# Two unused 32-byte tiles around the split x in SBUF

## The chip, the cores and the metric

The kernel runs on one core of a Trainium2 chip. The metric is the device time of one execution in microseconds (us), the median of several runs. Five engines work side by side, each through its own queue in order: TensorE (PE; its weight loads are shown apart as PEld), VectorE (DVE), ScalarE (ACT), GpSimd (POOL) and SyncE (SP), which here issues all the transfers. Data lies in SBUF, 128 partitions wide; "offset" below means the byte at which a tile begins in every partition. Products are accumulated in PSUM.

## The reference

One layer of a decoder trunk on x of 256 tokens by 1024 features, all in float32: an RMSNorm with gain, one projection to q, k, v and z, causal attention of 16 heads of 64 with ALiBi, a gate by silu(z), an output projection, the residual, and a final RMSNorm. With 256 tokens there is only one block of the block-sparse attention, so it is plain causal softmax attention.

```python
hn = rms_norm(x, norm_g)
q, k, v, z = split(hn @ w_in, 4)                 # 1024 x 4096
logits = (q . k) * 64**-0.5 - slope[h] * (t - s), masked where s > t
o = softmax(logits) @ v                          # 16 heads
h = x + (o * silu(z)) @ w_out                    # 1024 x 1024
out = rms_norm(h, final_g)
```

## The kernel before

Every dense product runs as three float32r products: an operand `a` is split into a high part `ah` and a low part `al`, and `a @ b` is taken as `ah@bh + ah@bl + al@bh`. x is transposed, multiplied by the gain and split once into `xh` and `xl` (tiles of 128 x 8 x 256, lines 121 and 122, written by `x_split`). The weights come in pieces of 1 MB through five buffers `rawt`; ACT casts a piece to its high part `wh` (line 439) and DVE subtracts that to give the low part `wl` (line 441), two units ahead of their use, into four buffers each.

The program is a list of dense units, which PE works through in order:

- v0: the first half of v, as its weights land (lines 348 to 350). Its stationary operand is xh or xl, its moving operand 512 columns of wh or wl.
- eight z units, "c" units (`cols_unit`, lines 198 to 200). Stationary: 128 columns of wh or wl. Moving: 256 columns of xh or xl. 24 products a unit.
- four v units (lines 224 to 226 by `rows_mm`), operands as in v0.
- sixteen c units, q and k of eight pairs of heads in turn. Beside them runs the attention.
- o1 and o2, the output projection (lines 224 to 226 again). Stationary: 128 columns of gh or gl, the split gated attention. Moving: wh or wl, 512 columns at a time, but for one 512-wide block of the second token tile, which is taken in two pieces of 256 columns (`PIECES`).

The work beside the dense products is put into the engines' queues at places given by the table `SCH`, in steps of a quarter unit. A pair's chain there is: q and k out of PSUM by DVE (`qf` line 237, `kf` line 251), split by ACT (lines 241, 255, 256) and DVE (lines 245, 260); scores on PE (`sc`, lines 281 and 283); softmax on DVE (line 291), ACT (298) and DVE (304, 306); transposes on PE (`pt`, 312) and copy by ACT (`pT`, 316); product with v on PE (`ot`, 324); gate on DVE (331), its split on ACT (334) and POOL (335). The two weight splits of a pair stand among these on ACT and DVE, in a fixed order. With `sc=12.47` the scores of pair 0 are issued after the first of four steps, so after six products, of the fourth q/k unit.

Tiles are placed in a pool one after the other, each rounded up to 32 bytes. The offsets in the two built programs:

| tile | before | modulo 64 | modulo 128 | after | modulo 64 | modulo 128 |
|---|---|---|---|---|---|---|
| xh, xl | 44224, 52416 | 0 | 64 | 44256, 52448 | 32 | 96 |
| gh, gl | 78048, 86240 | 32 | 96 | 78112, 86304 | 32 | 32 |
| wh, wl (first of four) | 139680, 156064 | 32 | 32 | 139744, 156128 | 32 | 96 |

All slices that the dense products take of these tiles begin at whole multiples of 512 bytes in them.

Of the kernel before, what the change touches and what calls it, by code (L numbers as in the profile page):

```python
# [8 lines left out]
F32 = mybir.dt.float32  # L9
# [9 lines left out]
P = 128  # L19
# [3 lines left out]
MASKED = 3.0e38  # L23
# Where the work beside the dense products is issued, in dense steps (four per unit) from the first step of a
# pair's q unit. ha, la, hb, lb: high and low parts of the weights of two units to come; hq .. lk: of q and k; sc: scores; per head sm: maximum and exponential, no: normalisation, pt: transpose,
# ph: its copy; pv: product with v; ga, gs: gate and its split.
SCH = dict(ha=1.26, la=3.94, hb=8.91, lb=9.56, hq=4.5, lq=5.61, hk=9.09, lk=10.02, sc=12.47, sm0=12.72, sm1=13.22,
           no0=14.14, no1=14.86, pt0=17.85, ph0=17.92, pt1=19.42, ph1=19.89, pv=20.6, ga=21.77, gs=23.88)
# column pieces of the output's 512-wide blocks, by token tile and block: the last one ends in a short piece
WHOLE = [slice(0, 512)]  # L30
# [4 lines left out]
def hybrid_trunk(ctx: ExitStack, tc: tile.TileContext, x, norm_g, w_in, w_out, final_g, out):  # L35
    """One MoBA layer over a single block (so causal ALiBi softmax attention), gated by silu(z).

    Dense products run as float32r passes: an operand a is split exactly into ah + al, each of
    12 significant bits, and a @ b = ah @ bh + al @ bh + ah @ bl, accumulated in float32.
    The pre-norm's 1/rms is a factor per token and is applied to the projections' outputs.  # L40
    Attention runs in plain float32.
    """
    nc = tc.nc
# [5 lines left out]
    one = ctx.enter_context(tc.tile_pool(name="one", bufs=1))  # L49
# [3 lines left out]
    sm = ctx.enter_context(tc.tile_pool(name="sm", bufs=4))  # L53
    ps = ctx.enter_context(tc.tile_pool(name="ps", bufs=1, space=bass.MemoryType.PSUM))
    ctx.enter_context(tc.manual_schedule())

# [1 line left out]
    xs = [one.tile([P, D], F32, name=f"xs{j}") for j in range(NS)]  # L58
# [7 lines left out]
    def load_cols(c, half):  # L66
        """Columns c*512 + half*256 .. +256 of w_in, all rows."""
        t = raw.tile([P, ND, 256], F32, name="rawt")
        raws[c, half] = t
        lo = c * 512 + half * 256  # L70
        nc.sync.dma_start(t, wi[:, :, lo:lo + 256])

    def load_rows(key, w, c, t0, n=4, step=2):
        """Row tiles t0 .. t0+n of columns c*512 .. +512."""
        t = raw.tile([P, 4, 512], F32, name="rawt")
        raws[key] = t
        for i in range(0, n, step):
            nc.sync.dma_start(t[:, i:i + step, :], w[:, t0 + i:t0 + i + step, c * 512:(c + 1) * 512])

# [1 line left out]
    warm = one.tile([P, 512], BF16, name="warm")  # L81
# [6 lines left out]
    nc.vector.memset(mhalf, -0.5)  # L88
    # dist[p, c] = 128 + p - c where c <= 128 + p, else huge
    dist = one.tile([P, S], F32, name="dist")  # L90
# [27 lines left out]

# [1 line left out]
    gps = ps.tile([P, ND], F32, name="gps", tag="pt", bufs=1)  # L120
    xh = one.tile([P, ND, S], F32R, name="xh")
    xl = one.tile([P, ND, S], F32R, name="xl")
    gT = one.tile([P, ND], F32, name="gT")
    rbc = one.tile([P, S], F32, name="rbc")
    zs = one.tile([P, ND, S], F32, name="zs")
    v = one.tile([P, NS, D], F32, name="v")
# [3 lines left out]

# [1 line left out]
    wps = ps.tile([P, 512], F32, name="wps", tag="ot", bufs=1)  # L132
# [6 lines left out]

# [1 line left out]
    xt = {}  # L141

    def x_transpose(j, b, i0=0, i1=4):
        """Row tiles 4b+i0 .. 4b+i1-1 of x's token tile j; neighbours in different PSUM banks."""
        for n in range(2):
            if i0 == 0:
                xt[j, b, n] = ps.tile([P, 2, P], F32, name="xt", tag="acc", bufs=4)
        for i in range(i0, i1):
            d = 4 * b + i
            nc.tensor.transpose(xt[j, b, i % 2][:, i // 2, :], xs[j][:, d * P:(d + 1) * P], ident)  # L150
# [23 lines left out]

# [1 line left out]
    wh, wl = {}, {}  # L176
# [12 lines left out]
    def split_rows(key, i, parts=1):  # L189
        """Row tiles 2i, 2i+1 of a half chunk."""  # L190
        return split((key, i), raws[key][:, 2 * i:2 * i + 2, :], [P, 2, 512], parts)

    held = {}       # accumulators that are read later
    late = []       # issued after the next unit's weight split

# [1 line left out]
    def mm3(acc, ah, al, bh, bl, start, stop):  # L197
# [20 lines left out]
    def rows_mm(acc, key, i, ah, al, t0, j, start, stop, cols=slice(0, 512)):  # L218
        """acc += (row tiles t0, t0+1 of the stationary operand) x (split piece)."""
        w_h, w_l = wh[key, i], wl[key, i]  # L220
        for n in range(2):
            lh = ah[:, t0 + n, j * P:(j + 1) * P]
            ll = al[:, t0 + n, j * P:(j + 1) * P]
            nc.tensor.matmul(acc, lh, w_h[:, n, cols], start=start and n == 0, stop=False)  # L224
            nc.tensor.matmul(acc, lh, w_l[:, n, cols], start=False, stop=False)  # L225
            nc.tensor.matmul(acc, ll, w_h[:, n, cols], start=False, stop=stop and n == 1)  # L226
            yield

    # q and k of a pair of heads (A in partitions 0-63, B in 64-127), split in two and laid out so that
    # one product over 128 partitions gives qh kh + ql kh and one over 64 gives qh kl  # L230
    qf, kf, qq, kk, kl = {}, {}, {}, {}, {}
# [38 lines left out]

# [1 line left out]
    sc, nl, mn, pe_, sums, rs, pn, pt, pT, ot = {}, {}, {}, {}, {}, {}, {}, {}, {}, {}  # L272

    def scores(p):
        """Heads A and B in turn, so that their products over 64 partitions can share the array."""
        for a in range(2):
            sc[2 * p + a] = ps.tile([P, 384], F32, name="sc", tag="sc", bufs=2)
        for o, q, k in ((slice(0, 128), slice(0, 128), slice(0, 128)),
                        (slice(128, 384), slice(128, 256), slice(0, 256))):
            for a in range(2):  # L280
                nc.tensor.matmul(sc[2 * p + a][:, o], qq[p][:, a, q], kk[p][:, a, k], start=True, stop=False)  # L281
            for a in range(2):
                nc.tensor.matmul(sc[2 * p + a][:, o], qq[p][HALF[a], a, q], kl[p][HALF[a], k], start=False, stop=True)  # L283
# [34 lines left out]
    def pv(p):  # L318
        """The two heads side by side, each in its half of the columns."""
        ot[p] = ps.tile([P, S], F32, name="ot", tag="ot", bufs=1)  # L320
        for j, o, q in ((0, slice(0, S), slice(0, S)), (1, slice(P, S), slice(S, 384))):
            for a in range(2):
                h = 2 * p + a
                nc.tensor.matmul(ot[p][HALF[a], o], v[:, j, h * DH:(h + 1) * DH], pT[h][:, q],  # L324
                                 start=j == 0, stop=j == 1)

    gated = {}
# [8 lines left out]

    # ================= schedule =================
    # v0: row tiles as they land
    accs = {}
    v0 = [(("v0", i // 2), i % 2) for i in range(4)]  # L340
# [39 lines left out]

    # the remaining pieces, in order of use
    units = []      # (name, arguments)
    for c, p0 in ((6, 0), (7, 4)):
# [30 lines left out]
    order = []  # L414
    for u in units:
        k = key_of(u)
# [13 lines left out]
    def split_u(u):  # L430
        """Split of unit u's weights in two steps: the high parts, then the low ones."""
        if u[0] == "c":
# [24 lines left out]
    def o_mm(n, i, half, j, m=0):  # L457
        """Row tiles 4 * half + 2i, + 1 into column piece m of output block (j, n)."""
        k = ("o1" if half == 0 else "o2", n)
# [6 lines left out]
    def dense(u):  # L466
        """One unit, in four steps."""
        if u[0] == "c":
# [13 lines left out]

    # what goes beside the dense steps, by position (four steps per unit)
    events = []
# [13 lines left out]
    gens = {}  # L498
    QK = 12     # the first pair's q unit
    for i in range(len(units) - 4):  # L500
# [54 lines left out]

# [1 line left out]
    do_split(units[-2])  # L557
# [4 lines left out]
    for j in range(NS):  # L562
# [3 lines left out]
        for t, (n, m) in enumerate(cuts):  # L566
# [6 lines left out]
            nc.vector.tensor_add(hh, acco[n, j, m][:, a], xs[j][:, c0:c1])  # L573
            # mean of squares + eps, piece by piece; a middle piece apart, on ACT
            if t == 2:
# [55 lines left out]
```

## Time and profile before

| what | value |
|---|---|
| time, median of 3 runs | 153.48 us (153.2 to 153.66) |
| profiled execution: span from first to last instruction | 151.4 us |
| median less that span | 2.1 us |
| PE busy | 142.8 us, 94% of the span, 1003 products |
| DVE busy | 108.0 us, 71% |
| ACT busy | 105.5 us, 70% |
| mean granted TensorE clock | 0.994 |

The page gives shares over the whole span, while the stages differ: x and v0 to 20.65 us, z units to 43.28, v units to 54.48, q/k units with attention to about 118, then o1, o2 and the last normalisation. For the profiled execution the span is what is measured; its time from launch to end isn't listed apart. A matmul's listed duration runs into that of the next, so the pace of a row of matmuls is read from the difference of their start times, not from their durations.

### The profile page before, as it was taken

The page shows a single profiled execution, that of the slowest core. Times are in us where ns is not written, and L with a number is a line of the kernel's source. Part 1 is how long each engine was busy: PE and PEld are TensorE (multiplying, and loading weights), DVE is VectorE, ACT ScalarE, POOL GpSimd, SP SyncE. Part 2 cuts the span into 40 slices and gives each one's busy share as a digit, 9 for nine tenths or more (in the row PEclk, how much of TensorE's full clock was granted, in tenths as well). Part 3 has the DMA queues.
Part 4 walks back from the last instruction along what each step waited for, and adds up shares of the span by engine and source line. Part 5 has one row for each costly group of instructions (what it writes and reads, how often), then busy time and mean ns, then how long its engine had stood idle before and what let it go on. Part 6 is the DMA issues. An engine that isn't in the chain of part 4 may idle for free.

```text
span 151.4 us, 2741 instructions
## 1 busy us (share of the span) xinstructions
PE 142.8 (94%) x1003; PEld 125.2 (83%) x1003; DVE 108.0 (71%) x262; ACT 105.5 (70%) x237; POOL 10.1 (7%) x20
## 2 busy tenths in 40 slices
PE   6889999999999999999999999999999999999930
PEld 4547899999988899999898989899898868787830
DVE  0447964864666307898998989898998979368771
ACT  3457996876676264998889797988889858560320
POOL 3000020000000000000010101010010101010210
PEclk9999999999999999999999999999999999999997
DMA  3899999999848600970458008440540000000033
GB/s 107 279 346 370 348 348 371 374 322 316 282 107 240 221 4 17 300 237 0 95 186 277 4 0 277 122 160 4 121 156 0 4 0 0 0 0 4 0 139 139
DMA packets 18332, 23.76 MB, mean 157 GB/s; under 512 B 648, under 2 KB 13584, under 8 KB 18320
## 3 DMA queue, kind: packets, MB, share of 16 engines
q1 hardware_dynamic: 18320, 23.60, 48.1%
q8 instruction: 8, 0.13, 0.3%
q14 instruction: 4, 0.03, 0.1%
HBM read 22.55 MB, written 1.05 MB: 156 GB/s over the span
## 4 chain that ended last, share of the span: by engine, by line
PE 78%; DVE 6%; issue 4%; DMA 4%; SPq 2%; ACT 2%; POOL 1%; POOLq 0%; DVEq 0%; ACTq 0%
PE accc L198 15%; PE accc L199 14%; PE accc L200 14%; DMA rawt<-in_w_in_dram 4%; PE ot L324 4%; PE acco L225 3%; PE acco L224 3%; PE acco L226 3%; PE pt L312 3%; PE sc L281 3%; PE sc L283 3%; PE accv L225 2%; PE accv L224 2%; PE accv L226 2%; DVE wl L441 2%
## 5 line engine op out<-in xcount | busy, mean ns | idle before, releaser
L198 PE MATMUL accc<-xh,wh 128*128 128x256 f32 x192 | 55.5, 289 | 0.0
L200 PE MATMUL accc<-xh,wl 128*128 128x256 f32 x192 | 53.6, 279 | 0.0
L199 PE MATMUL accc<-xl,wh 128*128 128x256 f32 x192 | 53.6, 279 | 0.0
L441 DVE TENSOR_TENSOR wl<-rawt,wh 128x1024 fp32r<-128x1024 f32 x36 | 43.8, 1220 | 13.5 <-ACT wh L439 10.8
L439 ACT CAST wh<-rawt 128x1024 fp32r<-128x1024 f32 x36 | 37.6, 1049 | 1.4 <-issue 1.1
L198 PEld LDWEIGHTS accc<-xh,wh 128*128 128x128 f32 x192 | 36.1, 188 | 1.2 <-issue 1.0
L199 PEld LDWEIGHTS accc<-xl,wh 128*128 128x128 f32 x192 | 36.1, 188 | 0.1
L200 PEld LDWEIGHTS accc<-xh,wl 128*128 128x128 f32 x192 | 36.1, 188 | 0.0
L298 ACT ACTIVATE nl<-nl,mn 128x128 f32<-128x128 f32 (+1 forms) x32 | 14.2, 445 | 2.0 <-DVE mn L291 1.5
L224 PE MATMUL acco<-wh,gh 128*128 128x512 f32 (+1 forms) x40 | 14.5, 362 | 0.0
L225 PE MATMUL acco<-wl,gh 128*128 128x512 f32 (+1 forms) x40 | 14.0, 350 | 0.3 <-DVE wl L441 0.3
L226 PE MATMUL acco<-wh,gl 128*128 128x512 f32 (+1 forms) x40 | 13.9, 348 | 0.0
L335 POOL TENSOR_TENSOR gl<-g,gh 128x256 fp32r<-128x256 f32 x8 | 6.0, 744 | 106.3 <-ACT gh L334 106.3
L306 DVE TENSOR_SCALAR nl<-nl,rs 128x128 f32<-128x128 f32 (+1 forms) x32 | 11.0, 386 | 0.6
L291 DVE CUSTOM_DVE_ANT_0 nl<-sc,bias 128x128 f32<-128x128 f32 (+1 forms) x32 | 9.5, 353 | 0.2 <-PE sc L283 0.2
L255 ACT CAST kk<-kf 64x256 fp32r<-64x256 f32 x16 | 6.5, 405 | 4.3 <-DVE kf L251 4.2
L225 PEld LDWEIGHTS acco<-wl,gh 128*128 128x128 f32 x40 | 7.5, 188 | 1.4 <-DVE wl L441 0.6
L224 PEld LDWEIGHTS acco<-wh,gh 128*128 128x128 f32 x40 | 7.5, 188 | 1.2 <-issue 0.3
L226 PEld LDWEIGHTS acco<-wh,gl 128*128 128x128 f32 x40 | 7.5, 188 | 1.1
L264 DVE TENSOR_TENSOR zs<-accc,rbc 128x256 f32<-128x256 f32 x8 | 3.4, 424 | 7.0 <-PE accc L200 6.4
L316 ACT COPY pT<-pt 128x384 f32<-128x384 f32 x16 | 6.9, 477 | 1.9 <-PE pt L312 1.9
L237 DVE SCALAR_TENSOR_TENSOR qf<-accc,rbc 128x256 f32<-128x256 f32 x8 | 3.4, 425 | 6.7 <-PE accc L200 6.5
(80 smaller groups left out, 217.3 us busy)
## 6 DMA issues: line engine op xcount, KB each, us to landing
rawt<-in_w_in_dram SPq DMA_DIRECT2D x12, 1024.0 KB, 6.8
rawt<-in_w_out_dram SPq DMA_DIRECT2D x8, 512.0 KB, 4.7
rawt<-in_w_in_dram SPq DMA_DIRECT2D x6, 512.0 KB, 8.4
rawt<-in_w_in_dram SPq DMA_DIRECT2D x4, 256.0 KB, 4.1
xs<-in_x_dram SPq DMA_DIRECT2D x3, 256.0 KB, 5.5
fg<-in_final_g_dram SPq DMA_DIRECT2D x1, 512.0 KB, 8.2
out_dram<-rawt SPq DMA_DIRECT2D x1, 512.0 KB, 2.6
out_dram<-rawt SPq DMA_DIRECT2D x2, 160.0 KB, 2.0
```

Of the source, the lines that this page charges most:

```text
L198: nc.tensor.matmul(acc, ah, bh, start=start, stop=False)
L199: nc.tensor.matmul(acc, ah, bl, start=False, stop=False)
L200: nc.tensor.matmul(acc, al, bh, start=False, stop=stop)
L224: nc.tensor.matmul(acc, lh, w_h[:, n, cols], start=start and n == 0, stop=False)
L225: nc.tensor.matmul(acc, lh, w_l[:, n, cols], start=False, stop=False)
L226: nc.tensor.matmul(acc, ll, w_h[:, n, cols], start=False, stop=stop and n == 1)
L291: nc.vector.tensor_tensor_reduce(nl[h][:, a], sc[h][:, a], bias[:, h, b], scale=1.0, scalar=3.0e38, op0=OP.add, op1=OP.min, accum_out=mn[h ...
L298: nc.scalar.activation(pe_[h][:, a], nl[h][:, a], AF.Exp, bias=mn[h][:, i:i + 1], scale=-1.0, accum_out=sums[h][:, i:i + 1])
L306: nc.vector.tensor_scalar(pn[h][:, a], pe_[h][:, a], rs[h][:, i:i + 1], None, op0=OP.mult)
L316: nc.scalar.copy(pT[h], pt[h])
L439: nc.scalar.copy(h_, src)
L441: nc.vector.tensor_sub(l_, src, h_.bitcast(F32))
```

## The change

Two tiles of 128 x 8 float32 (32 bytes a partition), `pad0` and `pad1`, are allocated right before `xh` and right after `xl`. Nothing writes or reads them. `xh` and `xl` begin 32 bytes later, everything allocated after them 64 bytes later. Comments are removed as well, and lines after 119 stand three lines further down. Each engine has the same instructions in the same order with the same waits.

```diff
     gps = ps.tile([P, ND], F32, name="gps", tag="pt", bufs=1)
+
+    one.tile([P, 8], F32, name="pad0")
     xh = one.tile([P, ND, S], F32R, name="xh")
     xl = one.tile([P, ND, S], F32R, name="xl")
+    one.tile([P, 8], F32, name="pad1")
     gT = one.tile([P, ND], F32, name="gT")
```

## Rows read from the trace of the kernel before

**Rows 1.** The page's 40 slices: busy tenths of three engines, and the granted clock.
```profile
PE   6889999999999999999999999999999999999930
DVE  0447964864666307898998989898998979368771
ACT  3457996876676264998889797988889858560320
PEclk9999999999999999999999999999999999999997
```

**Rows 2.** Groups by line and shape: count | busy us, mean ns | idle before.
```profile
L198 PE MATMUL accc<-xh,wh 128*128 128x256 f32 x192 | 55.5, 289 | 0.0
...
L224 PE MATMUL acco<-wh,gh 128*128 128x512 f32 x24 | 10.0, 416 | 0.0
...
L224 PE MATMUL accv<-wh,xh 128*128 128x512 f32 x16 | 6.3, 395 | 0.0
...
L224 PE MATMUL acco<-wh,gh 128*128 128x256 f32 x16 | 4.5, 282 | 0.0
```

**Rows 3.** Timeline of PE, z units: start us, us, engine, line, operation.
```profile
26.48 0.28 PE L198 MATMUL accc<-xh,wh 128*128 128x256 f32 x1
...
40.48 0.28 PE L198 MATMUL accc<-xh,wh 128*128 128x256 f32 x1
```

**Rows 4.** Timeline of PE, o2, pieces of 256 columns.
```profile
142.59 0.28 PE L226 MATMUL acco<-wh,gl 128*128 128x256 f32 x1
...
144.97 0.28 PE L226 MATMUL acco<-wh,gl 128*128 128x256 f32 x1
```

**Rows 5.** Timeline of PE, the v units' first product and the one after their last.
```profile
43.28 0.39 PE L224 MATMUL accv<-wh,xh 128*128 128x512 f32 x1
...
54.48 0.28 PE L198 MATMUL accc<-xh,wh 128*128 128x256 f32 x1
```

**Rows 6.** Timeline of PE, o2 at 512 columns, and the product after it.
```profile
134.19 0.40 PE L225 MATMUL acco<-wl,gh 128*128 128x512 f32 x1
...
142.36 0.28 PE L224 MATMUL acco<-wh,gh 128*128 128x256 f32 x1
```

**Rows 7.** Timeline of PE, a k unit beside the attention.
```profile
107.30 0.28 PE L199 MATMUL accc<-xl,wh 128*128 128x256 f32 x1
...
110.48 0.28 PE L199 MATMUL accc<-xl,wh 128*128 128x256 f32 x1
```

**Rows 8.** Timeline of PE and DVE at the scores of pair 0.
```profile
63.58 0.33 PE L281 MATMUL sc<-kk,qq 128*128 128x128 f32 x2
...
64.95 0.29 DVE L291 CUSTOM_DVE_ANT_0 nl<-sc,bias 128x128 f32<-128x128 f32 x1 [0.19 <-PE sc L283]
```

**Rows 9.** Waits from 66 to 121 us: engine line waited for: us, times, longest.
```profile
ACT kk L255 <- DVE kf L251: 3.3, 6, 0.6
DVE wl L441 <- ACT wh L439: 2.8, 6, 0.5
ACT gh L334 <- DVE g L331: 2.0, 6, 0.4
PEld accc L198 <- issue: 1.0, 6, 0.2
```

**Rows 10.** Timeline of DVE: the low weight part that waits, pairs apart.
```profile
80.11 1.23 DVE L441 TENSOR_TENSOR wl<-rawt,wh 128x1024 fp32r<-128x1024 f32 x1 [0.46 <-ACT wh L439]
...
113.97 1.23 DVE L441 TENSOR_TENSOR wl<-rawt,wh 128x1024 fp32r<-128x1024 f32 x1 [0.46 <-ACT wh L439]
```

**Rows 11.** Timeline of PE and ACT: the product with v, and the copy it needs.
```profile
72.49 0.43 PE L324 MATMUL ot<-pT,v 128*64 128x256 f32 x1
...
105.75 0.48 ACT L316 COPY pT<-pt 128x384 f32<-128x384 f32 x1
...
106.27 0.66 PE L324 MATMUL ot<-pT,v 128*64 128x256 f32 x4
```

**Rows 12.** Timeline of PE: where it waits for DVE at the attention's end.
```profile
121.93 0.50 PE L225 MATMUL acco<-wl,gh 128*128 128x512 f32 x1 [0.28 <-DVE wl L441]
```

**Rows 13.** Busy time by window, two pairs: PE, PEld, DVE, ACT, POOL; clock, DMA.
```profile
79.95:88.40 8.45, 8.45 (x73) 7.73 (x72) 7.78 (x23) 7.34 (x20) 0.75 (x1) 1.00 0.36 123
88.40:96.85 8.45, 8.45 (x73) 7.73 (x72) 7.78 (x23) 7.32 (x20) 0.74 (x1) 1.00 0.38 125
```

## The prediction

> **What bounds the kernel now.** I read the slices first: PE is busy in nine tenths or more of nearly every slice from 12 us to the tail, at the full clock, while DVE and ACT only come close to that in the second half [rows 1]. So up to about 60 us the pace of PE's products is the time, and after it three engines are near their limit at once. The question is then what one product costs, so I took start times from the timeline and not the listed durations.
>
> The c units take 14.00 us from 26.48 to 40.48, which is five units of 24 products: 116.7 ns a product of 256 columns [rows 3]. The o2 pieces of the same 256 columns take 2.38 us from 142.59 to 144.97, 21 products: 113.3 ns [rows 4]. At 512 columns the v units take 11.20 us for 48 products, 233.3 ns [rows 5], and o2 8.17 us for 35, 233.4 ns [rows 6]. There are 576 products in c units (192 on each of three lines) and 48 pieces of 256 columns in o1 and o2 [rows 2].
>
> Now put the offsets modulo 64 beside these paces, moving operand first. c units, 0 and 32: 116.7. o pieces of 256, 32 and 32: 113.3. v units, 32 and 0: 233.3 for 512. o at 512, 32 and 32: 233.4. So at 512 columns it makes no difference where the stationary operand begins; at 256 columns the one arrangement with equal offsets is 3.3 ns quicker than the one without. Shape, type and order of operands (two products share a stationary tile, two a moving one) are alike in both.
>
> Then the second half. Between 66 and 121 us the waits name only DVE on ACT and ACT on DVE, and PE on nothing but its own issue [rows 9]. The wl that waits for its wh comes at 80.11 and, four pairs on, at 113.97: 8.465 us a pair [rows 10]. PE's product with v comes at 72.49 and four pairs on at 106.27: 8.445 us a pair [rows 11]. Thus DVE and ACT, handing kf, kk, wh and wl to each other, go round in a ring that is already slightly slower than PE, though DVE's busy share is only 7.78 of 8.45 [rows 13]; its idle time is the 0.46 for wh. The lag ends at 121.93, where PE waits for a wl [rows 12]. The last time the ring waits for PE is at 64.95, for pair 0's scores [rows 8]; no wait after it is for PE.
>
> **The change part by part.** The two pads add no instruction and take none away, and xh and xl are 32 bytes further on. What can change is the pace of products that read them.
>
> v0 and v units, 96 products: xh and xl are the stationary operand, which goes from 0 to 32, with the moving one at 32. That is the arrangement of o at 512, which has the same pace to 0.1 ns [rows 5, 6]. Cost nothing; at the bounds ±0.1 ns times 96, 0.01 us.
>
> c units, 576 products: the moving operand goes from 0 to 32, the stationary one stays at 32. That is the arrangement of the o pieces, so 116.7 becomes 113.3, 80 ns a unit. The nearest rows on the other side are a k unit in which a stretch of 27 products took 3.18 us, 117.8 each, without any change of offsets [rows 7]: the pace has other states, so a worse one can't be excluded. I take 113.3, because its arrangement of offsets is the very one, and keep 117.8 and, one step of 3.3 in the other direction, 120.0 for the range.
>
> What of it reaches the end. Up to pair 0's scores PE's products are the path: eight z units, q and k of pair 0 and q of pair 1 make 11 units, and six products of the next unit precede the scores at 63.58. 270 products by 3.33 ns are 0.90 us. The ring starts 0.90 us earlier with that; DVE's work in front of it (kf and wl hang on k of pair 0, two units before) moves by 0.80, and it has 0.19 of idle there [rows 8], so it isn't late.
>
> After it the other 306 products would give PE up to another 1.0 us, about 0.15 a pair (some 45 of 48 products go back to back). I give that nothing. The ring's operations read rawt, wh, PSUM and small tiles, whose offsets modulo 64 are what they were, so it stays at 8.465 a pair, while PE would do with 8.30. PE can run ahead only by its lead on the ring, and the shortest is on pT: a copy ends at 106.23, and PE's group of four products that takes it begins at 106.27 and lasts 0.48 to the next group, with the second head's pair in its second half [rows 11], so some 0.3 us. Two pairs use that up. Then PE waits about 0.16 us a pair at the product with v, and at the end it waits for the same wl, 0.90 us earlier than at 121.93. From there on o1 and o2 are PE's, at paces that don't change, and everything moves by 0.90.
>
> Transposes, scores, softmax, transfers and POOL: all their tiles after the pads move by 64, alike modulo 64, so nothing. Raw weights land long before their use; a load that starts with a freed buffer starts earlier with it. The loads of the last two thirds leave the transfers largely idle (0.36 and 0.38 in two windows) [rows 13].
>
> Sum: span 151.4 − 0.90 = 150.5 us; with the 2.1 us between span and median, **152.6 us**.
>
> **The rivals.** *Offsets don't matter.* The quicker o pieces would be so for a reason of their own, as by where in the stream they stand. For it: at 512 columns equal and unequal offsets have one pace, and a c unit has been seen in two states [rows 7], so a pace alone isn't proof of an address. Against it: the o pieces hold 113.3 to the end of a run of 21, while no c unit that I looked at is under 116.7. Time 153.5. The Trainium skill speaks for this rival: SBUF — State Buffer, "Who interferes with whom", gives TensorE two read ports of its own, moving and stationary apart, and says it never waits on anyone; and its lines are 16 bytes, so 0 and 32 are equally good starts. By that page the sum is zero. The two paces at one shape show that something holds PE back which the page doesn't have.
>
> *A longer period than 64.* In the o pieces the two operands are equal modulo 64 but 64 apart modulo 128 (32 and 96); after the change xh and wh are equal modulo 128 too (96 and 96), which no stretch of before shows. If two streams that start in step collide there, the c units become slower: the place is the same 576 products, the price the step of 3.3 ns upwards. Then 270 by 3.33 is +0.90 to the first scores; after them PE's pair becomes 8.60, over the ring's 8.465, so PE bounds again, and of the 0.13 in each of six pairs all counts but its lead of some 0.3 and the 0.28 of its wait [rows 12]: +0.2 to +0.5. Time 154.6 to 154.9, I say 154.7. It decides against me as soon as the c pace is over 116.7; at 117.8 it would be 153.9.
>
> *PE's gain isn't capped.* Should the ring be held by PE in a way that the waits don't show, all 576 products count: 1.9 us, 151.6. Against it stand six periods of the ring without a wait for PE [rows 9].
>
> The skill's TensorE: Matmul & The Clock Gate, "Back-to-back issue gap", has 256/2.4 + 2.5 = 109.2 ns for 256 columns. As an estimate by that page, if equal offsets took away all of the excess, 270 products would give 2.0 us, 151.5; the trace is over that figure in every arrangement, the o pieces too, so I don't use it.
>
> **How the numbers follow.** The forecast gets 0.60: it has a direct model in the same kernel, but one of 48 products, and one reading of the address. Offsets don't matter: 0.22. A longer period: 0.14. Not capped: 0.04. A measurement of this kernel, whose three runs span 0.46 us, tells a difference from none at about 0.3%, 0.46 us. Faster than 153.02 are the forecast and the last, 0.64; the same 0.22; slower 0.14. The forecast's own range is 152.3 to 152.9. Taking in the case without effect with its scatter up to 153.7, and a little of a larger gain down to 152.2, holds 0.82.
>
> **What would show it.** In the new trace, starts of L198's products in the z units: 2.72 us a unit and not 2.80, 113.3 a product. The v units still 11.2 us. The first scores at about 62.7. Then 8.46 a pair from product with v to product with v, with new idle time of PE or PEld on pT or wl, and DVE's and ACT's waits for each other as before. PE's wait at the end near 121.0 and longer. I am wrong in the first step if the z units keep 2.80 or go above, and in the cap if a pair takes 8.3.

## The result, and the profile after

The changed kernel takes 154.39 us (22 runs, 153.56 to 158.16), the kernel before 153.55 (22 runs, 152.80 to 154.15). The ratio is 1.0053, 95% interval 1.0037 to 1.0068: half a per cent slower. Three runs of the changed kernel, 156.44 to 158.16, were in a slower state of the chip, and the ratio leaves them out. The forecast had it 0.6% faster; 154.39 is outside its range and on its other side. What came is the second rival, a longer period than 64.

The page first: PE's busy time, then the chain that ended last. Before the change PE was busy for 142.8 us, and its share of that chain was 78%, as the last line below shows, from the page of before.

```profile
PE 143.9 (95%) x1003; PEld 127.6 (84%) x1003; DVE 108.4 (72%) x262; ACT 105.5 (70%) x237; POOL 10.1 (7%) x20
...
PE 91%; issue 3%; DVE 2%; POOL 1%; POOLq 0%; DVEq 0%
```

```profile
PE 78%; DVE 6%; issue 4%; DMA 4%; SPq 2%; ACT 2%; POOL 1%; POOLq 0%; DVEq 0%; ACTq 0%
```

Timeline of PE (start us, us, engine, line): four z units, the v units with the product after them, and the 256-column pieces of o2. Lines stand three further down than before.

```profile
28.33 0.28 PE L201 MATMUL accc<-xh,wh 128*128 128x256 f32 x1
...
39.85 0.28 PE L201 MATMUL accc<-xh,wh 128*128 128x256 f32 x1
...
42.73 0.40 PE L227 MATMUL accv<-wh,xh 128*128 128x512 f32 x1
...
53.64 0.28 PE L201 MATMUL accc<-xh,wh 128*128 128x256 f32 x1
...
142.54 0.28 PE L229 MATMUL acco<-wh,gl 128*128 128x256 f32 x1
...
144.92 0.28 PE L229 MATMUL acco<-wh,gl 128*128 128x256 f32 x1
```

Read differences of starts. 96 c products take 11.52 us: 120.0 ns where it was 116.7 [rows 3]. The 48 v products take 10.91 us where it was 11.20 [rows 5]; most of them are at 226.7 ns, not 233.3. The o2 pieces, whose two operands moved together, keep their 113.3 [rows 4]. The granted clock was 1.00, the upper of its two levels, in the z and v units of both kernels, so the clock isn't what differs.

The second half, DVE's wl and PE's product with v four pairs apart:

```profile
79.54 1.23 DVE L444 TENSOR_TENSOR wl<-rawt,wh 128x1024 fp32r<-128x1024 f32 x1 [0.46 <-ACT wh L442]
...
113.78 1.23 DVE L444 TENSOR_TENSOR wl<-rawt,wh 128x1024 fp32r<-128x1024 f32 x1 [0.46 <-ACT wh L442]
```

```profile
72.04 0.76 PE L327 MATMUL ot<-pT,v 128*64 128x256 f32 x6
...
106.35 0.65 PE L327 MATMUL ot<-pT,v 128*64 128x256 f32 x4
```

A pair now takes 8.56 and 8.58 us; it was 8.465 and 8.445 [rows 10, 11]. DVE and ACT were the slower side by 0.02; now PE is. One hand-over shows it: DVE's wl, the maximum that DVE issues right behind it, and the last group of PE's scores that this maximum reads. First the changed kernel, then before:

```profile
88.06 1.22 DVE L444 TENSOR_TENSOR wl<-rawt,wh 128x1024 fp32r<-128x1024 f32 x1 [0.46 <-ACT wh L442]
...
88.88 0.39 PE L286 MATMUL sc<-kl,qq 64*128 64x256 f32 x2
...
89.30 0.29 DVE L294 CUSTOM_DVE_ANT_0 nl<-sc,bias 128x128 f32<-128x128 f32 x1
```

```profile
88.57 1.23 DVE L441 TENSOR_TENSOR wl<-rawt,wh 128x1024 fp32r<-128x1024 f32 x1 [0.46 <-ACT wh L439]
...
89.06 0.38 PE L283 MATMUL sc<-kl,qq 64*128 64x256 f32 x2
...
89.71 0.28 DVE L291 CUSTOM_DVE_ANT_0 nl<-sc,bias 128x128 f32<-128x128 f32 x1
```

In before the maximum starts 1.14 us after wl, in all pairs from the second to the seventh, and 0.65 after the scores. In the changed kernel it starts 1.24 after wl and 0.42 after the scores; by that much pair 0's maximum follows its scores in both kernels, where it waits for them. So from the fourth pair to the seventh DVE waits about 0.1 us a pair for PE, too little to be listed as a wait. These are the waits that are listed from 66 to 121 us, without POOL's (engine, line, us, times, longest):

```profile
ACT kk L258 <- DVE kf L254: 3.3, 6, 0.6
DVE wl L444 <- ACT wh L442: 2.8, 6, 0.5
ACT gh L337 <- DVE g L334: 2.0, 6, 0.4
PEld accc L201 <- issue: 1.0, 6, 0.2
ACT nl L301 <- DVE mn L294: 0.8, 4, 0.2
```

The first four rows are as before [rows 9], though another engine sets the pace. The new fifth row is the same lateness handed on, ACT waiting for DVE's maximum; it doesn't name PE. Neither rows that stay the same nor the new one name the bound; the period and the hand-over above do. PE's own 0.28 us wait at the attention's end [rows 12] is gone, and only PEld still has one, from 121 to 123 us:

```profile
PEld acco L228 <- DVE wl L444: 0.3, 1, 0.3
```

The stages, worked out from PE's start times (us). "Rest" runs from the last pair's scores to the span's end.

```
                                   before   after  c alone  v alone  x by 80
first c product at                  20.65   19.48    21.02    20.31    20.75
from it to the first v product      22.63   23.25    23.08    22.72    22.11
v units                             11.20   10.91    11.22    11.07    11.23
78 c products to pair 0's scores     9.10    9.35     9.29     9.17     8.92
pair 0's to the last pair's scores  58.92   59.43    59.21    58.92    58.95
rest                                28.90   28.92    28.98    29.00    28.89
span                               151.40  151.34   152.79   151.19   150.85
```

From the first c product on, the change costs 0.62 − 0.29 + 0.25 + 0.51 + 0.02 = 1.11 us. The profiled execution shows none of it in its span, since its c products began 1.17 us earlier. Some of that is v0: its last 30 products took 6.91 us, not 7.08, which for 48 makes about 0.3, an estimate. The remaining 0.9 is put down to when loads arrived: ACT's cast of a weight piece that it waits for began at 9.23 us, not 10.34, and in other kernels' profiles the first c product stands anywhere from 19.9 to 22.8. 1.11 − 0.3 = 0.8 us fits the medians, which differ by 0.84.

### The profile page after: what moved, and what is told of

Read it like the earlier page. It is cut to its first block, busy times and chain, and to the rows that moved or that the text cites. A ratio compares the mean times of both kernels' runs of the same rounds, so it can differ in the third digit from the quotient of the medians.

```text
span 151.3 us, 2741 instructions
## 1 busy us (share of the span) xinstructions
PE 143.9 (95%) x1003; PEld 127.6 (84%) x1003; DVE 108.4 (72%) x262; ACT 105.5 (70%) x237; POOL 10.1 (7%) x20
## 4 chain that ended last, share of the span: by engine, by line
PE 91%; issue 3%; DVE 2%; POOL 1%; POOLq 0%; DVEq 0%
PE accc L201 16%; PE accc L203 15%; PE accc L202 15%; PE ot L327 4%; PE acco L227 4%; PE acco L228 4%; PE acco L229 4%; PE pt L315 3%; PE sc L284 3%; PE sc L286 3%; PE acc L351 3%; PE acc L353 3%; PE wps L139 2%; PE acc L352 2%; PE accv L227 2%
## 5 line engine op out<-in xcount | busy, mean ns | idle before, releaser
L201 PE MATMUL accc<-xh,wh 128*128 128x256 f32 x192 | 56.1, 292 | 0.0
L203 PE MATMUL accc<-xh,wl 128*128 128x256 f32 x192 | 54.3, 283 | 0.0
L202 PE MATMUL accc<-xl,wh 128*128 128x256 f32 x192 | 54.3, 283 | 0.0
L201 PEld LDWEIGHTS accc<-xh,wh 128*128 128x128 f32 x192 | 36.7, 191 | 1.2 <-issue 1.0
L202 PEld LDWEIGHTS accc<-xl,wh 128*128 128x128 f32 x192 | 36.8, 192 | 0.1
L203 PEld LDWEIGHTS accc<-xh,wl 128*128 128x128 f32 x192 | 36.8, 192 | 0.0
L158 ACT ACTIVATE xh<-xt,gT 128x128 fp32r<-128x128 f32 x16 | 5.3, 376 | 4.2 <-PE xt L153 4.2
```

What stands on the lines that cost most here:

```text
L201: nc.tensor.matmul(acc, ah, bh, start=start, stop=False)
L202: nc.tensor.matmul(acc, ah, bl, start=False, stop=False)
L203: nc.tensor.matmul(acc, al, bh, start=False, stop=stop)
```

## The experiments

"Distance" is where the moving operand begins less where the stationary one does. Modulo 256 it is 32 in before's c units, 224 in v, 192 in o; after the change 0, 0 and 192.

**Other pads, at distances 192 and 0.** The edit is shown against the changed kernel.

```diff
-    one.tile([P, 8], F32, name="pad1")
+    one.tile([P, 24], F32, name="pad1")
```

> xh and xl begin where the change puts them (offset 96 modulo 128), but the second pad is 96 bytes, so the weights stand at 32 modulo 128, as in the kernel before: moving less stationary is 64 in the c units. Theory A (the pace of a product is set by the distance of the two operands modulo 128; 64 is the best for 256 columns, 0 the worst): z units 2.72 us (113.3 ns a product), v units 11.2 us as before; DVE's and ACT's ring keeps 8.465 us a pair; 0.9 us under the kernel before. Theory B (xh's own place decides; at 96 modulo 128 it reads slowly): z units 2.88 us and v units 10.9 us as with the change, about 0.8 us over the kernel before.

Ratio 1.0017 (0.9983 to 1.0052). The z units took neither pace; two products four units apart:

```profile
28.14 0.28 PE L200 MATMUL accc<-xh,wh 128*128 128x256 f32 x1
...
39.45 0.28 PE L200 MATMUL accc<-xh,wh 128*128 128x256 f32 x1
```

That is 117.8 ns. But from the ninth product of the first unit to its end, and beside the attention from shortly after the product with v to the next transposes, c units ran at 113.3: one distance, two paces. The o pieces show the same at an unchanged 192: the first group in o1 ran at 113.3, the others, in o1 and o2, at 118, where before had 113.3 in all. Beside the attention this kernel is the test of the ring. The product with v, the copies that it takes, and the first product after its group; then the last two in before:

```profile
79.25 0.85 ACT L318 COPY pT<-pt 128x384 f32<-128x384 f32 x2
...
80.02 1.00 PE L326 MATMUL ot<-pT,v 128*64 128x256 f32 x8
...
80.95 0.38 PE L200 MATMUL accc<-xh,wh 128*128 128x256 f32 x1
```

```profile
80.93 0.87 PE L324 MATMUL ot<-pT,v 128*64 128x256 f32 x8
...
81.73 0.39 PE L198 MATMUL accc<-xh,wh 128*128 128x256 f32 x1
```

The group takes 0.93 us, and 0.85 to 0.95 in the first six pairs; in before it has 0.80 in every pair. The 48 c products between two groups take 0.07 to 0.16 us less, and a pair still takes 8.44 on average. ACT's two copies end at 80.10, after PE's group has begun. So PE waits for pT, and DVE and ACT keep the period.

The 24 floats in `pad0` instead put both operands elsewhere and back at distance 0:

> Pads of 96 and 32 bytes: xh at 32 modulo 128, the weights at 32: distance 0 as with the change, but both operands elsewhere. Theory A: as with the change, z units 2.88 us, v units 10.9 us, 0.5% over the kernel before. Theory B (xh's own place): another pace than 2.88 us a z unit.

Ratio 1.0085 (1.0056 to 1.0114). Two z products four units apart:

```profile
28.92 0.28 PE L200 MATMUL accc<-xh,wh 128*128 128x256 f32 x1
...
40.44 0.28 PE L200 MATMUL accc<-xh,wh 128*128 128x256 f32 x1
```

That is 120.0, and v has 227: as with the change. It is not one operand's own place: the kernel with pads of 32 and 96 has xh where the change has it, and its weights where this kernel has them, modulo 256, and runs at another pace than both.

**Everything by 32 bytes** (one pad ahead of all tiles).

> One pad of 32 bytes ahead of every tile: all distances stay, all offsets modulo 64 change from 0 to 32 or from 32 to 0. Theory A: every pace as before (z unit 2.80, v units 11.2 us, o pieces 113.3 ns), no difference in time. Theory B, or a theory by which the other engines or the transfers feel the offset: paces or times move.

The ratio is 1.0011 (0.9986 to 1.0035); z units take 2.80 us and o pieces 113.3 ns, as before.

**Products alone.**

> No layer is computed: groups of 48 float32r products, in threes as in the dense units, stationary operand at 32 modulo 128, the moving one 0, 16, ... 112 bytes further on modulo 128 (letters a to h), at 256, 512 and 128 columns; then groups of bf16. Theory A: at 256 columns 120.0 ns a product at a, 116.7 at c and g, 113.3 at e; at 512 columns 226.7 at a, 233.3 at c, e and g. Theory B (the moving operand's own place, 96 modulo 128 slow): 256 columns slowest at e, which stands at 96, and c, which stands at 64, at 116.7. If neither operand's place matters and the order in the stream does: one pace for all letters.

These are settled paces in ns from start times, by distance. 256 columns: 113.3 at 16 and 112 bytes, 116.7 at 32, 118.3 at 48, 117.8 at 64, 120.0 at 80 and 96; the row at 0 waited for data. 512 columns: 226.7 at 0, 231.6 at 16, 233.3 at 32, 48 and 96, 228.9 at 64, 231.1 at 80 and 112. 128 columns: 111.7 at all. bf16, two starts 45 products apart:

```profile
229.76 0.27 PE L70 MATMUL btwoa<-mob,stb 128*128 128x256 bf16 x1
...
234.67 0.27 PE L70 MATMUL btwoa<-mob,stb 128*128 128x256 bf16 x1
```

That is 109.1 ns, and the three rows at other distances have the same. So of the two types float32r alone has the excess. A float32r product of 128 columns takes 111.7, hardly less than one of 256, so at 128 it isn't the columns that set the pace; no run shows what does. The Trainium skill, TensorE: Matmul & The Clock Gate, "Back-to-back issue gap", has N / 2.4 + 2.5 ns for an isolated product, which as an estimate for 256 columns is 109.2; the bf16 rows agree, no float32r row does.

**One part alone.** The split weights of a unit are placed inside wider tiles (shortened):

```diff
+OFF = {'v0': 8, 'v': 8, 'c': 0, 'o0': 0, 'o1': 0}      # v alone; c alone has c 8, the third c 4
+    def part(name, shape, off):
+        t = spl.tile([P, 1056], F32R, name=name)
+        return t[:, off:off + 1024].rearrange("p (a s) -> p a s", s=shape[2])
```

> The kernel before, its weight buffers 128 bytes wider; in v0 and v units the weights are put 32 bytes into the buffer, so that these 96 products stand at distance 0 modulo 128, all others as before. Theory A (the distance sets the pace): 226.7 ns a product in place of 233.3, v units 10.9 us, z units 2.80 as before; 0.3 us less for the v units, up to 0.3 more for v0 as far as its transfers let it: 0.3 to 0.6 us faster. If v0 waits for its weights anyway: 0.3.

> As the run above, but the c units' weights are put 32 bytes into their buffers and no others: the 576 products of 256 columns at distance 0, v0 and v as before. Theory A: 120.0 ns a product, z units 2.88 us, pairs 8.58 us as with the change, so 0.9 us more up to the first scores and 0.5 to 0.7 after them: 1.3 to 1.6 us slower, more than the change.

The ratio with v alone is 0.9984 (0.9962 to 1.0006), with c alone 1.0063 (1.0035 to 1.0091). So the c units make it slower. What v gives back isn't clear of the noise in the medians; the table above has it, 11.07 us for 11.20. Both tests are blurred. A tile is 4224 bytes here, so every other unit stands 128 further modulo 256, which I had not thought of: with c alone, units took 2.88 and 2.84 us in turn.

> The c units' weights 16 bytes into their buffers: distance 16, the other products as before. Theory A: 113.3 ns a product, as the groups at that distance had: z units 2.72 us, pairs 8.465 us by the ring of DVE and ACT: 0.9 us faster. Theory C (the distance only allows several paces, and how a run of products begins picks one): some units at 113.3, others at 117 or more, a gain of less than 0.9.

The ratio is 1.0086 (1.0057 to 1.0115), with units at 117.4 to 119.8: the opposite of what was expected. This kernel has the same tiles of 4224 bytes, and weights that begin at 16 modulo 32.

**After which entry, and with which period.**

> No layer is computed: groups of 24 products of 256 and 12 of 512 columns at distances 0, 16, ... 112 modulo 128 (letters a to h), each three times, after one, two and three transposes (x, y, z). Theory A: one pace per letter whatever the number of transposes: at 256 columns 120.0 at a, f and g, 113.3 at b and h, 116.7 to 118.4 at c to e. Theory C: at some letters, e above all, two paces, by the entry.

After other entries, 16 held 116.8 or 118.7 and 64 held 113.3 or 117.8; 0 went to 120.0, 32 to 116.7 and 112 to 113.3 (within 15 products) every time.

> No layer: rows of 24 products of 256 columns and 12 of 512, two rows at each distance of moving behind stationary operand, 0 to 240 bytes in steps of 16 (letters a to p), and of 256 columns at 256, 288, 320 and 384 (q, r, s, t); transposes in front of each row. Theory A (the distance counts modulo 128): letters i to p repeat a to h, i 120.0 as a, k 116.7 as c. Theory B (it counts modulo 256, since the kernel with c alone at distance 0, whose tiles of 4224 bytes put every other unit at 128, had units of 119.8 and of 118.5 ns in turn): i about 118.5, not 120.0; q, r, s, t as a, c, e, i. Theory C (a longer period still): q, r, s differ from a, c, e too.

The letters q to t stood in fact at 1024, 1152, 1280 and 1536 bytes. 128 gave 118.2 and 119.1; q, s and t 120.0, as at 0; r 118.2, with the pattern of 128. So 128 bytes is too short a period, and all of it fits 256.

> No layer: c units alone, in the layer's own order (wh by xh, wh by xl, wl by xh over eight row tiles of 512 and 1024 bytes) and at the layer's own addresses of xh, wh and wl; xh and xl begin 0 to 496 bytes later in steps of 16, so that their distance behind the weights runs over all multiples of 16 modulo 512 (d288 is before's, d0 and d256 stand for the changed kernel's). Two units in a row after one transpose (x), and again after two (y). Theory A (the steps of operands from product to product set the pace with the distance, which is why 112 gave 113.3 in rows with steps of 1024 and 2048 bytes and 120.0 in the layer): units here repeat the layer's paces, 116.7 at 288, 120.0 at 256 and 0, 120.0 at 112, and 117.8 at 192; some distances hold 113.3 after either entry, or none does. Theory B (only what ran before a unit chooses the pace): x and y differ at most distances, and the layer's paces aren't repeated.

Three distances, read up to the second unit, where the pace has settled, with 24, 21 and 21 products between the rows:

```profile
146.29 0.28 PE L75 MATMUL d112x<-xh,wh 128*128 128x256 f32 x1
...
149.01 0.28 PE L75 MATMUL d112x<-xh,wh 128*128 128x256 f32 x1
```

```profile
106.13 0.28 PE L75 MATMUL d0x<-xh,wh 128*128 128x256 f32 x1
...
108.65 0.28 PE L75 MATMUL d0x<-xh,wh 128*128 128x256 f32 x1
```

```profile
117.30 0.28 PE L75 MATMUL d32x<-xh,wh 128*128 128x256 f32 x1
...
119.75 0.28 PE L75 MATMUL d32x<-xh,wh 128*128 128x256 f32 x1
```

That is 113.3, 120.0 and 116.7 ns. Over all 32 distances, d and d + 256 run alike where one pace holds after both entries. Neither theory is whole: address and entry both choose (192: 117.8, and its partner 448 113.3 or 117.8), and of the sixteen only 112 settled at 113.3 every time here. All these rows have stationary operands at whole multiples of 32 bytes.

**Distance 112 in the layer, by the weights.** Tiles of 4608 bytes, c 44 floats on.

> The split weights of c units begin 176 bytes later in tiles of 4608 bytes, so that xh and xl lie 112 bytes behind them modulo 128 and modulo 512; v0, v, o1 and o2 stay as before. This gives the c units the pace that the forecast took for the change and so tests its remaining steps. Theory A (the pace follows the distance, and the ring of DVE and ACT caps the gain): at 112 every row of products without a layer fell to 113.3 ns, after up to 14 products at 116 to 121; so z units of 2.72 to 2.76 us, some 0.8 us to the first scores, then still 8.46 us a pair with PE waiting at the product with v; 152.7 us against 153.5. Theory B (every break in a unit starts the slower pattern again): z units at 2.78 or more, time as before, 153.3 to 153.5. Theory C (PE's gain isn't capped): 151.7, pairs of 8.3 us.

```profile
28.64 0.28 PE L202 MATMUL accc<-xh,wh 128*128 128x256 f32 x1
...
40.16 0.28 PE L202 MATMUL accc<-xh,wh 128*128 128x256 f32 x1
```

That is 120.0 ns, and the ratio is 1.0086 (1.0051 to 1.0120), 154.74 us: no theory has both the pace and the time. The next kernel has this and v and the first output block at distance 0:

> As the kernel with c at 112, and v0 and v at distance 0 (32 bytes on) and the first 512-wide output block at distance 0 (64 bytes on). If paces by distance are all there is: c as in that kernel, about -0.8 us; v and v0 -0.25 us, as these two measured alone; 48 products of 512 columns of o1 and o2 from 233.4 to 227 ns, -0.3 us behind the ring's last wait: 152.1 us against 153.5. If the gains of v0 are lost to loads and those of o1 to the wait for the last weights: 152.5. If the distances of units disturb each other: no better than c at 112 alone.

The ratio is 1.0070 (1.0040 to 1.0100), with c at 120.0, v at 227, and o at 227 only in stretches.

**The same distance by xh and xl.**

```diff
-    xh = one.tile([P, ND, S], F32R, name="xh")
+    xh = one.tile([P, 2304], F32R, name="xh")[:, 20:2068].rearrange("p (a s) -> p a s", s=S)
```

> xh and xl begin 80 bytes later in wider tiles (9216 bytes, so that nothing else moves modulo 1024); the weights stay where they begin before, at 32 modulo 64. c units are at distance 112 as in the kernel that moved the weights by 176 bytes and stayed at 120.0 ns a product. Theory A (where the stationary operand begins counts too: there the weights began at 16 modulo 32, here and in the rows without a layer they don't): z units of 2.72 to 2.76 us, first scores 0.8 us earlier, then pairs of 8.46 us with PE waiting at the product with v; 152.7 to 152.9 us against 153.6, less if the v units, whose stationary xh now begins at 16 modulo 32, lose up to 4 ns on each of 96 products (0.4). Theory B (the layer around it chooses 120 at this distance): z units of 2.88, 154.6 as there.

```profile
28.92 0.28 PE L198 MATMUL accc<-xh,wh 128*128 128x256 f32 x1
...
39.80 0.28 PE L198 MATMUL accc<-xh,wh 128*128 128x256 f32 x1
...
63.01 0.33 PE L281 MATMUL sc<-kk,qq 128*128 128x128 f32 x2
...
121.39 0.50 PE L225 MATMUL acco<-wl,gh 128*128 128x512 f32 x1 [0.33 <-DVE wl L441]
```

That is 113.3 ns, with a ratio of 0.9958 (0.9935 to 0.9981), as theory A has it. The first scores come 0.57 us earlier [rows 8], though the first c product began 0.10 later, and the wait for the last wl comes 0.54 earlier and is about as long [rows 12]: what is won before the ring is kept, and nothing is added to it. There was little to add: between two products with v the 48 c products take 5.87 us where before has 5.89, since the pace hardly settles between the breaks there.

> As the kernel with xh and xl 80 bytes on, and the weights of v0 and v 112 bytes on in tiles of 4608 bytes, so that they are at distance 0 from xh (both then begin at 16 modulo 32). Theory A: c as in that kernel (113.3), v at 227 ns and 0.3 us less than before's 11.20 in the v units, as at distance 0 with aligned operands: 152.4 to 152.6 us. Theory A': stationary operands at 16 modulo 32 have other paces, so v stays at 231 or more: 152.7 to 153.1. Theory B: z units of 2.88 and 154.3 us.

The ratio is 0.9946 (0.9927 to 0.9965), at 152.72 us the quickest of all, though its interval overlaps the one before. c has 113.3; v stayed at 233.3 at distance 0, with the stationary xh at 16 modulo 32, where tiles at multiples of 32 had 227.

## Why the prediction was wrong, point by point

- *"That is the arrangement of the o pieces, so 116.7 becomes 113.3"* is the step that failed. Offsets modulo 64 were read as the property. The distance counts modulo 256: the o pieces are at 192, the changed c units at 0, and 0 settles at 120.0 in this kernel, in two other layers and in rows without a layer. Even the model pace wasn't the o pieces' own: at 192 they ran at 113.3 or at 118.
- *The bound of 120.0, "one step of 3.3 in the other direction"*, and the rival's place and price per product were what came. Its period of 128 was too short, and its 154.7 us was 0.3 high; it too put v0 and v at nothing. That the bound was the pace to come is luck: one step upwards was taken without a row that had it.
- *v0 and v "cost nothing"*: wrong in size, −0.29 us for v and about −0.3, an estimate, for v0. The two rows it rested on [rows 5, 6] stood at 224 and 192, where 512 columns happen to have one pace; 0 has another. With it the sentence fell that at 512 columns the stationary operand's start makes no difference.
- *The ring caps a gain at 8.465 us a pair*: held. Distance 192 showed the period kept with PE waiting, x by 80 that an early start is kept to the end. In the other direction there is no cap: PE's pair went to 8.58, DVE's maximum waited for PE's scores, and a pair of the ring grew by about 0.1.
- *270 products by 3.33 are 0.90*: too large even at 113.3. x by 80 won 0.67 from the first c product to the first scores, as some 10 to 16 products behind each break run at about 118 before the pace settles.
- *Offsets don't matter*, for which the Trainium skill spoke (SBUF — State Buffer, "Who interferes with whom": TensorE never waits on anyone): they do here. One shape has 113.3, 116.7 and 120.0 ns with nothing changed but where tiles begin. Whether anything waits for a port in it is not shown.

How a distance makes its pace stays open; no run looks inside the array. So does why 112 with weights at 16 modulo 32 runs at 120.0; that the odd start does it is a guess, as it was tried in two layers, not by itself.

## What to carry to other kernels

Before a pace is put down to an address, compare two places that differ in that address alone; two stretches of one kernel differ in more residues than the one you look at. A microbenchmark of products in the layer's own order, over all distances, is one run and finds the arrangement to try; then measure it in the layer with either operand moved, for here moving xh and xl gave the pace and moving the weights didn't. And before adding up a gain per product, find the last wait that decides: up to the ring each product that settles counts, after it none. A loss counts after it too, once it is larger than the slack.

## What was not expected of the hardware

float32r products of 256 columns settle at paces between 113.3 and 120.0 ns, often at 113.3, 116.7, 117.8, 118.3 or 120.0. With stationary operands at multiples of 32 bytes the pace goes by the distance of the two operands modulo 256 bytes, at some distances also by what ran before; bf16 has 109.2 at the four distances tried. The best and the worst lie 16 bytes apart (96: 120.0, 112: 113.3). Equal starts, which the change gives the c and v units, are among the worst for 256 columns (120.0) and the best for 512 (226.7 against 233.3).
